# First mixer of a two-layer trunk: the convolution's input in PSUM, one of its blocks in the first pass, fourteen taps on ScalarE

## The chip, the core and the metric

One NeuronCore of a Trainium2 chip. The metric is the device time of one execution in microseconds (us). Five engines run side by side, each through its own instructions in order: TensorE (PE, matmuls), VectorE (DVE), ScalarE (ACT), GpSimd (POOL) and SyncE (SP), whose queue issues the DMA loads. SBUF holds operands; PSUM holds what TensorE writes, in eight banks of 128 partitions by 512 floats.

## The reference, cut to what matters

Two layers over 256 tokens of width 2048. Each layer: a modulation vector, a mixer, an output projection, a feed-forward network. The change lies in the mixer of layer 0:

```python
def even_mixer(h, ...):
    z = h @ w_in
    a, q, kc, vc, ks, vs, kw, vw, gl = split_cols(z, EVEN_SPLITS)
    y_a = conformer_conv(a, conv_w, conv_b, conv_ln_g, conv_ln_b)
    y_b = nsa_attention(q, kc, vc, ks, vs, kw, vw, gl, cos, sin, positions, ...)
    return jnp.concatenate([y_a, y_b], axis=-1) @ w_out

def conformer_conv(a, w_dw, b_dw, ln_g, ln_b):
    a1, a2 = jnp.split(a, 2, axis=-1)
    y = causal_dwconv(a1 * jax.nn.sigmoid(a2), w_dw, b_dw)     # 31 taps, one filter per channel
    return jax.nn.silu(layer_norm(y, ln_g, ln_b))
```

The attention has 8 query heads of 128 in 2 groups; queries and keys are normalised (a root per head and token), scaled and rotated (rope). `mod = silu(c) @ ada_w + ada_b` gives the modulation.

## The kernel before

**Tiles.** The contraction over 2048 runs as 16 tiles of 128 (`kt`). Weights come through three SBUF buffers named `raw`, in the order in which `W.want` listed them; `W.take` hands out the next and loads ahead. In the first mixer all products are fp32; such a product shows as two records in the trace.

**The first pass** (the loop over `kt` at the end of the setup) makes, for each `kt`, the compressed keys' input (`oc`, 2 products of 256 columns), the keys (`ok`) and the first four query heads for both key groups (`oq`), 6 products of 512 columns. Two rows of the modulation matrix (`ada`, 1 MB each) are loaded and reduced on VectorE beside each `kt`.

**After it**, in program order: four *fills*, two products `ev_v` (values and gate logits), two `ev_c` (the compressed values' input), a compression network `hidden(0)`, two fills, `hidden(1)`, and then attention with nine more fills and one spare take. A fill is one 256-column projection over all 16 `kt`, half of a convolution block; a *pair* of fills is a block of 128 channels, of which there are 8. The first fill of a pair goes through `tanh` on ScalarE into `sg`; with the second, `taps` writes the gated block `xp = (sg + 1) * o`, padded by 30 columns.

**The convolution.** Block `c` has 31 taps, in jobs of four VectorE taps (`PER`). ScalarE multiplies `TAPS_ACT` of the 31 shifted views by their weights into `pr`, GpSimd adds these into `yp`; VectorE accumulates the others into `y` and `ye`. `xp` lies in SBUF, in two buffers. Every `take` runs `hook` (the next step of attention or of the heads) and `tick`, which emits jobs and modulation rows by the rates `CONV_*` and `ADA_*`. The position of each in the engines' streams is thus set when the program is built, and each engine goes through its stream in order.

**The heads.** `squares(i)` sums the squares of the keys (i = 0) and of the two halves of the first four heads' banks on ScalarE, `roots` takes the 24 roots at once on VectorE, `scaled(i)` multiplies, `roped(i)` rotates (two of four steps on GpSimd, `rope`'s `rest` on VectorE), `turned_in(i)` transposes on TensorE (L613) into `KT` and `qT`, from within `ev_v`.

**Attention**, for head `hd`: scores (L1142, L1145), their maxima on VectorE (`weights`, L1157 to L1165), exponentials on ScalarE, the factors of the sums (L1179 to L1182), transposes (L1194), copies to SBUF (`pT` L1198 on VectorE, L1199 and L1200 on ScalarE), the product with the values (L1205, L1209). Three heads are under way at a time, each step a hook, and half a fill lies between the steps.

**The end of the mixer** (`out_first`): projection with the weights `out`, first over the attention's half of the mix; meanwhile the convolution's last blocks are finished, `centre` and `layer_stats` (L986, L987) and `layer_scale` (L408, L409) give its layer norm, and then the convolution's half follows. The modulation rows go through two buffers `ada`: the load of row n waits in SP's queue until VectorE has reduced row n - 2, and the weight loads behind it wait with it.

Of the kernel before, what the change touches and what calls it, by code (L numbers as in the profile page):

```python
# [16 lines left out]
P = 128  # L17
# [29 lines left out]
TAPS_ACT = 10  # L47
TAPS_LAST = 9
# [6 lines left out]
LO_A = 0.25  # L55
ADA_A = 0.25
CONV_A = 0
CONV_1 = 0.7
CONV_2 = 2.0
CONV_3 = 1.2  # L60
# [8 lines left out]
ADA_T = 0.4  # L69
LO_F = 0.25  # L70
ADA_1 = 0.5
ADA_2 = 0.5
ADA_3 = 0.6
# [6 lines left out]
ADA_OUT = 0.45  # L80
# [72 lines left out]
def trunk(ctx, tc, a, out):  # L153
# [9 lines left out]
    psum = ctx.enter_context(tc.tile_pool(name="psum", bufs=8, space=bass.MemoryType.PSUM))  # L163

    def bank():
        return psum.tile([P, 512], F32, tag="bank", name="bank")

# [39 lines left out]
    for kt in range(KD):  # L207
        W.want(a["ev_1"][kt], 1, 1792, cuts=(768, 1024), split=False)
# [9 lines left out]
    want_pairs(0, 2)  # L218
    for c in range(2):
        W.want(a["ev_v"][c], KD, 268, split=False)  # L220
    for g in range(2):
        W.want(a["ev_c"][g], KD, P, split=False)
    want_hidden(0)
    want_pairs(2, 3)
    want_hidden(1)
    want_pairs(3, 8)
# [506 lines left out]
    V.memset(onesm, 1.0)  # L733
    make_identity(nc, ident)
# [38 lines left out]
    oc = [bank()[:, :T] for _ in range(2)]  # L773
    ok = [bank() for _ in range(NT)]
    oq = [[bank() for _ in range(NT)] for _ in range(2)]
    for kt in range(KD):
        x = h(kt)
        if kt > 1:
            next(table, None)
        first, stop = kt == 0, kt == KD - 1  # L780
        w, _ = take()
        for g in range(2):
# [14 lines left out]
    with tc.tile_pool(name="l0", bufs=2) as lp:  # L797
# [84 lines left out]
        xps = [lp.tile([P, 30 + T], F32, name=f"xp{u}", bufs=1) for u in range(2)]  # L882
        for xp in xps:
            G.memset(xp[:, :30], 0.0)
# [3 lines left out]
        def fill():  # L888

            o = proj_t(h)  # L890
# [130 lines left out]
        def roots():  # L1021
            flat = s24.rearrange("p a b -> p (a b)")
            V.tensor_scalar(flat, flat, 1.0 / P, EPS, op0=ALU.mult, op1=ALU.add)
            r = rsqrt(flat, 24)
            V.tensor_scalar(r[:, 8:], r[:, 8:], SCALE, None, op0=ALU.mult)
            root.append(r)

        def scaled(i):
# [3 lines left out]
            for t in range(NT):  # L1032
                u = 2 * i + t
                head_scale(zs[u], 4, root[0][:, 4 * u:4 * u + 4], gain, n[:, t])
# [21 lines left out]
        hooks.append(lambda: (squares(0), adds[0]()))  # L1056
        hooks.append(lambda: (squares(1), adds[1]()))
        hooks.append(lambda: (squares(2), masks()))
        hooks.append(roots)
        hooks.append(lambda: scaled(0))  # L1060
        hooks.append(lambda: (scaled(1), roped(0)))
        hooks.append(lambda: (scaled(2), roped_rest()))
        hooks.append(lambda: roped(1))
        hooks.append(lambda: (turned_in(0), roped_rest()))
        hooks.append(lambda: roped(2))
        hooks.append(lambda: (turned_in(1), roped_rest()))
        hooks.append(None)
        hooks.append(lambda: turned_in(2))
        rate.update(ada=ADA_A, jobs=CONV_A)
        W.share = LO_A  # L1070
        for _ in range(4):
            fill()
# [14 lines left out]


# [5 lines left out]
        for g in range(2):  # L1094
            o = proj_t(h)
            defer(lambda g=g, o=o: hooks.append(windows(1, g, o)))
# [142 lines left out]
        for _ in range(9):  # L1239
# [10 lines left out]
        def ready(c):  # L1250
# [3 lines left out]
            if c < 7:  # L1254
# [4 lines left out]
                                      lambda: (normed(1), activated(0))], ready, ADA_OUT)  # L1259

# [233 lines left out]
def layout(inputs):  # L1494
# [51 lines left out]
    a["ev_1"] = np.concatenate([s["kc"], s["ks"], s["kw"], s["q"]], axis=1).reshape(KD, P, 1792)  # L1546
# [45 lines left out]
```

## Time and profile before

| what | us |
|---|---|
| median of 3 runs | 2399.79 (2398.73 to 2402.48) |
| the profiled execution, and its span | 2407.39, 2405.7 |
| TensorE busy in the span | 2305.6 (96%) |
| first pass on TensorE | 31.62 to 140.96 |
| from there to the first scores | 140.96 to 286.15 |
| attention, to the first product of `out` | 286.15 to 386.49 |
| end of the mixer, to the feed-forward network | 386.49 to 516.53 |

TensorE is busy nearly all of the span, so the places of interest are those where it waits, and the stretches after such waits in which its matmuls take longer. In a list of the instructions in order of time, the value in brackets at a row's end is how long the engine stood idle just before it, and behind the arrow who ended that; merged rows give a count (x), and the duration covers all of them.

### The profile page before, as it was taken

Reading aid. Unit: us, or ns where it says so; the run is one execution under the profiler, and the core shown is the slowest. Engines: PE = TensorE matmul, PEld = TensorE weight load, DVE = VectorE, ACT = ScalarE, POOL = GpSimd, SP = SyncE. Lnnn points to the kernel's source line nnn. Section 1 sums busy time; section 2 is a strip of 40 time slices with the busy share of each in tenths; the row PEclk is TensorE's granted clock in tenths of the full one; section 3 lists DMA queues with packets and bytes.
Section 4 is the critical chain, followed back from the end, with each engine's and each line's share of the span. In section 5 each row is a group of like instructions: output and inputs, shape, how many; then the busy total and the mean of one; then the engine's idle time right before and its main releaser. Section 6 shows DMA issues by size and latency. Waiting matters only on the chain. (4 is left out here: it accounts for less than half of the span.)

```text
span 2405.7 us, 39971 instructions
## 1 busy us (share of the span) xinstructions
PE 2305.6 (96%) x16056; PEld 2133.9 (89%) x16056; DVE 1669.6 (69%) x2611; ACT 1028.5 (43%) x1803; POOL 527.5 (22%) x309
## 2 busy tenths in 40 slices
PE   6898999998999999999999999999999999999999
PEld 3476777888999999999999877999999999999999
DVE  7758689738968877877888467665686554554554
ACT  2021254125434544544544555446534444444443
POOL 4233534001312222222222010000222212222221
PEclk9999999999999999999999999999999999999999
DMA  9968754866878888878887543444577545545545
GB/s 381 427 223 340 291 192 175 294 237 258 322 282 330 331 298 333 328 289 312 333 316 269 199 175 123 153 175 167 217 276 266 187 157 203 184 159 205 181 166 168
DMA packets 96381, 596.62 MB, mean 248 GB/s; under 512 B 11457, under 2 KB 14145, under 8 KB 44097
## 3 DMA queue, kind: packets, MB, share of 16 engines
q1 hardware_dynamic: 96194, 594.06, 66.6%
q8 instruction: 126, 2.06, 0.3%
q14 instruction: 61, 0.50, 0.1%
HBM read 591.92 MB, written 2.10 MB: 247 GB/s over the span
## 5 line engine op out<-in xcount | busy, mean ns | idle before, releaser
L133 ACT ACTIVATE whi<-raw 128x1024 fp32r<-128x1024 f32 (+2 forms) x659 | 626.1, 951 | 856.1 <-PE bank L347 716.2
L139 DVE TENSOR_TENSOR wlo<-raw,whi 128x1024 fp32r<-128x1024 f32 (+1 forms) x515 | 585.4, 1138 | 410.2 <-ACT whi L133 409.8
L348 PE MATMUL bank<-h,wlo 128*128 128x256 f32 x2624 | 745.0, 284 | 12.3 <-DVE wlo L139 11.4
L346 PE MATMUL bank<-h,whi 128*128 128x256 f32 x2624 | 744.8, 284 | 0.2 <-ACT whi L133 0.2
L347 PE MATMUL bank<-h,whi 128*128 128x256 f32 x2624 | 743.8, 283 | 0.0
L139 POOL TENSOR_TENSOR wlo<-raw,whi 128x1024 fp32r<-128x1024 f32 (+2 forms) x144 | 339.9, 2360 | 1484.0 <-ACT whi L133 1439.5
L348 PEld LDWEIGHTS bank<-h,wlo 128*128 128x128 f32 x2624 | 505.0, 192 | 14.0 <-DVE wlo L139 12.6
L346 PEld LDWEIGHTS bank<-h,whi 128*128 128x128 f32 x2624 | 505.2, 193 | 0.5 <-ACT whi L133 0.5
L347 PEld LDWEIGHTS bank<-h,whi 128*128 128x128 f32 x2624 | 505.2, 193 | 0.1
L269 DVE CUSTOM_DVE_ANT_0 ada<-ada,cB,adab 128x2048 f32<-128x2048 f32 x192 | 464.9, 2425 | 29.6 <-DMA ada<-adaw 28.9
L347 PE MATMUL bank<-g,whi 128*128 128x256 f32 x1408 | 403.7, 287 | 9.7 <-DVE g L662 9.6
L346 PE MATMUL bank<-g,whi 128*128 128x256 f32 x1408 | 403.4, 287 | 7.6 <-ACT g L661 7.2
L348 PE MATMUL bank<-g,wlo 128*128 128x256 f32 x1408 | 404.1, 287 | 5.5 <-DVE wlo L139 4.1
L347 PEld LDWEIGHTS bank<-g,whi 128*128 128x128 f32 x1408 | 274.6, 195 | 11.3 <-DVE g L662 11.3
L346 PEld LDWEIGHTS bank<-g,whi 128*128 128x128 f32 x1408 | 274.7, 195 | 8.6 <-ACT g L661 7.8
L348 PEld LDWEIGHTS bank<-g,wlo 128*128 128x128 f32 x1408 | 274.7, 195 | 8.1 <-DVE wlo L139 5.4
L350 PE MATMUL bank<-hw,raw 128*128 128x256 f32 x640 | 150.6, 389 | 13.1 <-DMA raw<-ev 7.5
L350 PEld LDWEIGHTS bank<-hw,raw 128*128 128x128 f32 x640 | 121.9, 194 | 42.3 <-issue 18.6
L650 DVE SCALAR_TENSOR_TENSOR y<-bank,fcw,y 128x255 f32<-128x255 f32 x162 | 77.4, 478 | 96.8 <-ACT y L649 96.8
L350 PE MATMUL bank<-hr,raw 128*128 128x257 f32 x640 | 140.4, 380 | 0.0
L350 PEld LDWEIGHTS bank<-hr,raw 128*128 128x128 f32 x640 | 121.0, 190 | 16.6
L350 PE MATMUL bank<-mixw,raw 128*128 128x256 f32 x512 | 119.0, 396 | 5.5 <-DMA raw<-out 5.5
(263 smaller groups left out, 2469.9 us busy)
## 6 DMA issues: line engine op xcount, KB each, us to landing
ada<-adaw SPq DMA_DIRECT2D x192, 1024.0 KB, 5.7
raw<-wup SPq DMA_DIRECT2D x162, 1024.0 KB, 6.3
raw<-wdn SPq DMA_DIRECT2D x128, 704.0 KB, 4.3
raw<-out SPq DMA_DIRECT2D x44, 512.0 KB, 3.6
raw<-ev_a SPq DMA_DIRECT2D x16, 1024.0 KB, 5.4
raw<-ev SPq DMA_DIRECT2D x16, 896.0 KB, 14.7
raw<-wup SPq DMA_DIRECT2D x16, 896.0 KB, 4.6
raw<-cmp_w SPq DMA_DIRECT2D x8, 1024.0 KB, 9.2
```

The lines of the kernel that those rows point to most:

```text
L133: nc.scalar.activation(hi[:, :n], raw, AF.Copy)
L139: eng.tensor_sub(lo[:, :n], raw, hi[:, :n].bitcast(F32))
L269: V.tensor_tensor_reduce(w, w, cB, 1.0, adab[:, i * 96 + j:i * 96 + j + 1], ALU.mult, ALU.add, m)
L346: PE.matmul(o, hi[:, s_], x[:, 0], start=start, stop=False)
L347: PE.matmul(o, hi[:, s_], x[:, 1], start=False, stop=False)
L348: PE.matmul(o, lo[:, s_], x[:, 0], start=False, stop=stop)
L350: PE.matmul(o, w[:, s_], x, start=start, stop=stop)
L650: V.scalar_tensor_tensor(y[:, 1:], o[:, :T - 1], w[:, 1:2], y[:, 1:], op0=ALU.mult, op1=ALU.add)
```

## The change

- The first pass makes one convolution block too: its weights (`ev_1`) are 2048 columns wide, not 1792, and `oc` has four parts, two of the compressed keys and two of a pair of fills. These lie two to a bank, so a bank is first set by a product of zeros. The first of the two banks comes from a new pool `xq` of one bank; the other seven are `psum0`.
- `xp` is one buffer in the bank of `xq`, no longer two in SBUF: `taps` of block c waits until the jobs of block c - 1 are all emitted, and both VectorE and ScalarE read the taps from PSUM.
- 14 taps of each block go to ScalarE and GpSimd (12 for the last), where it was 10 (9); VectorE has 17 (19) instead of 21 (22).
- The roots are taken by parts (`roots(0)`, `roots(1)`, `roots(2)`), the keys' at once after the first pass.
- After the first pass come `ev_c`, `ev_v` with the transposes, `hidden(0)`, one pair, `hidden(1)`, and twelve fills around and beside attention. `W.load_to(kt + 2)` puts the load of a pass's weights ahead of that iteration's modulation rows in SP's queue.
- Rates of jobs and modulation rows are other numbers. After the mixer `all_banks` gives the feed-forward network eight banks again.

```diff
-TAPS_ACT = 10
-TAPS_LAST = 9
+TAPS_ACT = 14
+TAPS_LAST = 12
...
-CONV_1 = 0.7
-CONV_2 = 2.0
-CONV_3 = 1.2
+CONV_1 = 0.6
+CONV_2 = 1.0
+CONV_3 = 2.0
...
-    psum = ctx.enter_context(tc.tile_pool(name="psum", bufs=8, space=bass.MemoryType.PSUM))
+    banks = [tc.tile_pool(name="xq", bufs=1, space=bass.MemoryType.PSUM),
+             tc.tile_pool(name="psum0", bufs=7, space=bass.MemoryType.PSUM)]
+    xq, psum = [p.__enter__() for p in banks]
...
-        W.want(a["ev_1"][kt], 1, 1792, cuts=(768, 1024), split=False)
+        W.want(a["ev_1"][kt], 1, 2048, cuts=(1024, 1024), split=False)
...
-    oc = [bank()[:, :T] for _ in range(2)]
+    oc = [xq.tile([P, 512], F32, tag="xp", name="oc"), bank()]
+    for o in oc:
+        PE.matmul(o, zero[:, :P], zero, start=True, stop=False)
+    oc = [o[:, u * T:(u + 1) * T] for o in oc for u in range(2)]
...
     for kt in range(KD):
+        W.load_to(kt + 2)
         x = h(kt)
...
-        for g in range(2):
-            mm_t(oc[g], w, slice(g * P, (g + 1) * P), x, first, stop)
-        mm_n(ok, w, slice(256, 768), x, first, stop)
+        for g in range(4):
+            mm_t(oc[g], w, slice(g * P, (g + 1) * P), x, False, stop and g % 2 == 1)
+        mm_n(ok, w, slice(512, 1024), x, first, stop)
...
-            while c > 1 and c - 2 not in tapped:
+            while c and c - 1 not in tapped:
                 jobs.pop(0)()
-            xp = xps[c % 2]
+            if not xps:
+                xps.append(xq.tile([P, 512], F32, tag="xp", name="xp")[:, :30 + T])
+                V.memset(xps[0][:, :30], 0.0)
+            xp = xps[0]
...
+        fill(oc[2])
+        fill(oc[3])
+        advance()
+        squares(0)
+        advance()
+        roots(0)
+        scaled(0)
+        hooks.append(lambda: squares(1))
+        hooks.append(lambda: (roots(1), scaled(1)))
+        hooks.append(lambda: (squares(2), adds[0]()))
+        hooks.append(lambda: (roots(2), scaled(2)))
...
-        for _ in range(9):
+        for _ in range(11):
             fill()
...
+    drain()
+    all_banks()
```

Three places in the engines' streams. In the rows `hw` is the layer's input, `raw` a weight buffer, `n` the scaled keys or heads.

TensorE, from the end of the first pass to the first compression network, before:

```order
L361 MATMUL bank<-raw,hw 128x512 x6
L350 MATMUL bank<-hw,raw 128x256 x64
L613 MATMUL bank<-ident,n 128x128 x8
L361 MATMUL bank<-raw,hw 128x268 x8
L613 MATMUL bank<-ident,n 128x128 x8
L361 MATMUL bank<-raw,hw 128x268 x10
L613 MATMUL bank<-ident,n 128x128 x8
L361 MATMUL bank<-raw,hw 128x268 x46
L350 MATMUL bank<-hw,raw 128x256 x32
```

The same stretch after:

```order
L366 MATMUL bank<-raw,hw 128x512 x6
L355 MATMUL bank<-hw,raw 128x256 x32
L366 MATMUL bank<-raw,hw 128x268 x22
L618 MATMUL bank<-ident,n 128x128 x8
L366 MATMUL bank<-raw,hw 128x268 x6
L618 MATMUL bank<-ident,n 128x128 x8
L366 MATMUL bank<-raw,hw 128x268 x4
L618 MATMUL bank<-ident,n 128x128 x8
L366 MATMUL bank<-raw,hw 128x268 x32
```

The 64 products of four fills are gone from here and 32 of `ev_c` stand in their place; behind them 22 products of `ev_v` come ahead of the first transposes, where there were none.

VectorE, the first taps beside attention, with the engines that each instruction waits for, before:

```order
L904 SCALAR_TENSOR_TENSOR xp_581<-sg,bank 128x256 [waits PE_49]
L926 TENSOR_SCALAR cy<-xp_581,cvw 128x256 [waits DVE_49]
L928 TENSOR_SCALAR ye<-xp_581,cvw 128x256
L930 SCALAR_TENSOR_TENSOR cy<-xp_581,cvw,cy 128x256 [waits DVE_49]
L930 SCALAR_TENSOR_TENSOR ye<-xp_581,cvw,ye 128x256 [waits DVE_49]
L930 SCALAR_TENSOR_TENSOR cy<-xp_581,cvw,cy 128x256 [waits DVE_49]
```

The same place after, on VectorE and then on ScalarE:

```order
L918 SCALAR_TENSOR_TENSOR xp<-sg,bank 128x256 [waits PE_49]
L940 TENSOR_SCALAR cy<-xp,cvw 128x256 [waits DVE_49,Activation_49]
L942 TENSOR_SCALAR ye<-xp,cvw 128x256
L944 SCALAR_TENSOR_TENSOR cy<-xp,cvw,cy 128x256 [waits DVE_49]
L944 SCALAR_TENSOR_TENSOR ye<-xp,cvw,ye 128x256 [waits DVE_49]
L944 SCALAR_TENSOR_TENSOR cy<-xp,cvw,cy 128x256 [waits DVE_49,Activation_49]
```

```order
L933 ACTIVATE yp<-xp,cvw 128x256 [waits DVE_49]
L933 ACTIVATE pr<-xp,cvw 128x256 [waits Pool_49] x2
L933 ACTIVATE pr<-xp,cvw 128x256 [waits DVE_49,Pool_49]
L933 ACTIVATE pr<-xp,cvw 128x256
L933 ACTIVATE pr<-xp,cvw 128x256 [waits Pool_49]
```

The first tap of every four on VectorE now waits for ScalarE, and the first of every three on ScalarE for VectorE, where only the writing of `xp` was waited for.

VectorE, the end of the layer norm in `out_first` (`layer_stats`, then `layer_scale`), before:

```order
L402 SCALAR_TENSOR_TENSOR rsy<-rst,rsy 128x2
L994 TENSOR_TENSOR mz<-mz,rsy 128x2
L408 TENSOR_SCALAR diag<-ident,rsy 128x128 x2
L408 TENSOR_SCALAR diag<-ident,mz 128x128 x2
L1005 TENSOR_TENSOR cy<-cy,bank 128x256
```

After:

```order
L407 SCALAR_TENSOR_TENSOR rsy<-rst,rsy 128x2
L1008 TENSOR_TENSOR mz<-mz,rsy 128x2
L274 ISA ada,mod<-ada,cB,adab 128x2048
L274 ISA mod 128x1
L413 TENSOR_SCALAR diag<-ident,rsy 128x128 x2
L413 TENSOR_SCALAR diag<-ident,mz 128x128 x2
```

A modulation row moved in between the roots and the diagonals that TensorE takes.

## Rows read from the trace of the kernel before

**Rows 1.** Waits of TensorE, 20 to 520 us: total, times, longest

```profile
PE bank L350 <- DMA raw<-ev: 7.5, 9, 1.2
PE bank L866 <- DVE hs L861: 3.0, 1, 3.0
PE bank L613 <- DVE n L606: 2.6, 2, 2.2
PE bank L849 <- DMA raw<-cmp_w: 2.2, 2, 1.5
PE bank L361 <- DMA raw<-ev_v: 1.6, 1, 1.6
PE bank L350 <- DMA raw<-ev_c: 1.5, 1, 1.5
```

**Rows 2.** TensorE in order of time, first pass: start, duration, engine, instruction, [idle before]

```profile
31.62 2.07 PE L350 MATMUL bank<-hw,raw 128*128 128x256 f32 x4 [3.54 <-ACT hw L511]
...
40.79 1.03 PE L350 MATMUL bank<-hw,raw 128*128 128x256 f32 x4
...
134.94 1.03 PE L350 MATMUL bank<-hw,raw 128*128 128x256 f32 x4
...
140.96 27.79 PE L350 MATMUL bank<-hw,raw 128*128 128x256 f32 x128
```

**Rows 3.** First pass, busy us by engine; last three columns: clock, DMA share, GB/s

```profile
40.00:125.00 85.00, 77.42 (x202) 37.30 (x201) 69.43 (x82) 8.91 (x16) 35.47 (x21) 1.00 1.01 426
```

**Rows 4.** TensorE in order of time, behind the last of the heads' transposes

```profile
182.99 19.92 PE L361 MATMUL bank<-raw,hw 128*128 128x268 f32 x84
```

**Rows 5.** VectorE in order of time: root step, modulation row, scalings, rope step

```profile
151.75 0.18 DVE L397 TENSOR_SCALAR rsi<-s 128x24 int32<-128x24 int32 x1
...
154.21 2.34 DVE L269 CUSTOM_DVE_ANT_0 ada<-ada,cB,adab 128x2048 f32<-128x2048 f32 x1
...
156.82 6.29 DVE L596 SCALAR_TENSOR_TENSOR n<-bank,rsy,gains 128x128 f32<-128x128 f32 x24
163.02 0.68 DVE L605 TENSOR_TENSOR n<-n,cc 128x512 f32<-128x512 f32 x1
```

**Rows 6.** ScalarE in order of time, ahead of the second compression network's turn

```profile
270.86 0.51 ACT L919 ACTIVATE pr<-xp,cvw 128x256 f32<-128x256 f32 x1 [2.22 <-POOL yp L921]
```

**Rows 7.** VectorE in order of time, taps and one head's step beside attention

```profile
293.52 0.94 DVE L930 SCALAR_TENSOR_TENSOR cy<-xp,cvw,cy 128x256 f32<-128x256 f32 x1
...
303.50 0.48 DVE L930 SCALAR_TENSOR_TENSOR cy<-xp,cvw,cy 128x256 f32<-128x256 f32 x1
303.89 0.48 DVE L930 SCALAR_TENSOR_TENSOR ye<-xp,cvw,ye 128x256 f32<-128x256 f32 x1
...
312.61 0.68 DVE L1198 COPY pT<-bank 128x512 f32<-128x512 f32 x1
...
316.71 0.48 DVE L930 SCALAR_TENSOR_TENSOR cy<-xp,cvw,cy 128x256 f32<-128x256 f32 x1
```

**Rows 8.** ScalarE in order of time, two copies out of PSUM

```profile
305.64 0.36 ACT L1199 ACTIVATE pT<-bank 128x256 f32<-128x256 f32 x1
305.90 0.36 ACT L1200 ACTIVATE pC<-bank 15x256 f32<-15x256 f32 x1
```

**Rows 9.** TensorE in order of time, attention

```profile
313.34 1.25 PE L1209 MATMUL bank<-pT,vn 128*128 128x128 f32 x8 [2.98 <-DVE pT L1198]
314.38 5.26 PE L350 MATMUL bank<-hw,raw 128*128 128x256 f32 x16
...
342.06 1.08 PE L1142 MATMUL bank<-KT,qT 128*128 128x271 f32 x4
...
365.08 1.08 PE L1142 MATMUL bank<-KT,qT 128*128 128x271 f32 x4
```

**Rows 10.** TensorE in order of time, end of the mixer

```profile
414.19 13.51 PE L350 MATMUL bank<-mixw,raw 128*128 128x256 f32 x48 [3.36 <-DMA raw<-out]
430.61 0.56 PE L986 MATMUL bank<-onesm,cs 128*128 128x1 f32 x2 [2.91 <-DVE cs L979]
```

More of the change, by code (lines that the diff above doesn't have):

```diff
@@ L68 @@
 LO_T = 0.25
-ADA_T = 0.4
+ADA_T = 0.6
 LO_F = 0.25
-ADA_1 = 0.5
-ADA_2 = 0.5
-ADA_3 = 0.6
+ADA_1 = 0.45
+ADA_2 = 0.45
+ADA_3 = 0.55
 ADA_F0S = 0.45
@@ L79 @@
 CONV = 1.6
-ADA_OUT = 0.45
+ADA_OUT = 0.55
 LO_L1 = 0.0
@@ L216, in want_hidden @@
             W.want_raw(a["cmp_w1"][kv, :, u * 2048:(u + 1) * 2048], 2048)
-    want_pairs(0, 2)
+    for g in range(2):
+        W.want(a["ev_c"][g], KD, P, split=False)
     for c in range(2):
         W.want(a["ev_v"][c], KD, 268, split=False)
-    for g in range(2):
-        W.want(a["ev_c"][g], KD, P, split=False)
     want_hidden(0)
-    want_pairs(2, 3)
+    want_pairs(1, 2)
     want_hidden(1)
-    want_pairs(3, 8)
+    want_pairs(2, 8)
     want_out(0)
@@ L733, in trunk @@
     V.memset(onesm, 1.0)
+    zero = hm.tile([P, 512], F32, tag="hm", name="zero")
+    V.memset(zero, 0.0)
     make_identity(nc, ident)
@@ L881, in trunk, with fill @@
         glu = []
-        xps = [lp.tile([P, 30 + T], F32, name=f"xp{u}", bufs=1) for u in range(2)]
-        for xp in xps:
-            G.memset(xp[:, :30], 0.0)
+        xps = []
         norm = {}
         count, totals, tapped = [0], [], set()
-        def fill():
-            o = proj_t(h)
+        def fill(o=None):
+            if o is None:
+                o = proj_t(h)
             if count[0] % 2 == 0:
@@ L1033, in scaled @@
                 u = 2 * i + t
-                head_scale(zs[u], 4, root[0][:, 4 * u:4 * u + 4], gain, n[:, t])
+                head_scale(zs[u], 4, root[i][:, 4 * t:4 * t + 4], gain, n[:, t])
         later = []
@@ L1054, in turned_in @@
                     S.activation(qT[i - 1][:, :, t * P:(t + 1) * P], p, AF.Copy)
[L1056 to L1072, printed above, removed]
         rate.update(ada=ADA_1, jobs=CONV_1)
         W.share = LO_1
+        fill(oc[2])
[9 more added lines that the diff above has]
+        hooks.append(lambda: (roots(2), scaled(2)))
+        hooks.append(lambda: (roped(0), adds[1]()))
+        hooks.append(lambda: (roped_rest(), roped(1)))
+        hooks.append(lambda: (roped_rest(), roped(2)))
+        hooks.append(lambda: (roped_rest(), masks()))
+        beside.extend([None] * 9)
+        for i in range(3):
+            beside.append(lambda i=i: turned_in(i))
         vn = lp.tile([P, NT, 536], F32, name="vn", bufs=1)
@@ L1086, in gates @@
             V.tensor_scalar(g_, g_, 1.0, None, op0=ALU.add)
+        for g in range(2):
+            o = proj_t(h)
+            defer(lambda g=g, o=o: hooks.append(windows(1, g, o)))
         for c in range(2):
```

23 lines of the change are left out of this document (11 added, 12 removed).

## Prediction

> **What bounds the kernel now.** I read the list of TensorE's waits first, then the instructions of each engine in order of time around each wait. TensorE does the same work before and after, but for two products of zeros: each convolution block still costs two fills, wherever they stand. So the change is worth only what it does to TensorE's idle time and to the slower matmuls that follow it, nearly all of it in the first mixer, up to 516 us. The waits of that part [rows 1] fall into four kinds: weights of the first pass (7.5 us in 9 waits), weights of the products behind it (2.2 + 1.6 + 1.5), VectorE's rotated keys and heads (2.6), and VectorE's or ScalarE's lateness around the convolution (3.0 in rows 1, 2.98 in rows 9, 2.91 in rows 10, with 3.36 for the weights `out`).
>
> What a wait costs beyond itself is read from what follows it. The 128 records from 140.96 take 27.79 us [rows 2], so 16 take 3.5 and 48 take 10.4. Behind the wait of 2.98, 16 took 5.26 [rows 9], 1.8 more; behind the wait of 3.36, 48 took 13.51 [rows 10], 3.1 more. I take 2 us for each wait of about 3.
>
> **First pass.** One 256-column product is 27.79 / 64 = 0.43 us, so a pair of fills is 32 x 0.43 = 13.9 us, and that much leaves the stretch behind the pass. It comes back as two products in each of 16 steps. A step without a wait takes 140.96 - 134.94 = 6.02 us [rows 2]; now 6.9. From 31.62 a pass that never waits would end at 31.62 + 16 x 6.9 + 3.1 = 145.1, where 3.1 is what the first step lost (40.79 - 31.62 = 9.17 against 6.02). The products of zeros stand in the 3.54 idle ahead of it and may save that: 142.0. The DMAs are full in this stretch, 426 GB/s at a share of 1.01 [rows 3], and 2.1 MB more to bring take 4.9 us: 145.9 if they set the end. But loading ahead of the modulation rows gives each step's weights a whole step more. I take 143.9, so 2.9 later with 13.9 less behind: **-11**. Ends: -13 (142.0) and -7 (nothing gained by the new order, every product behind the DMAs).
>
> **Keys and heads.** After the pass TensorE has 13.9 us of `ev_c` and 22 products of 268 columns (0.45 each by width) until it wants the keys, 23.8 us after the pass. It was 27.6 us of fills before the first transposes. VectorE now passes, counted from the end of the pass: three root chains of 12, 13 and 13 steps at 0.2 (7.6), 24 scalings at 0.262 (6.3), eight taps (3.2), two additions for the compression (about 1 each), two modulation rows (4.7), the keys' rope (4 x 0.65 = 2.6) [rows 5, 7]. That is 26.4, so keys 2.6 late; GpSimd beside it can make that 4, if it slows a rope step as it slows taps [rows 7]. The first heads need 4 taps and a rope more and come as they are wanted; the second need another 4 taps, a modulation row and a rope (6.5) while TensorE has about 3.7 us of work: 2.5 late. With slower matmuls behind two waits that is 8 to 9, against 2.6 and about 1 (84 records of 268 columns took 19.92 [rows 4], 19.1 by width) before: **+4.5**, ends +2 and +8.
>
> **Weights behind the pass.** `ev_c` is now partly loaded before the pass ends, and less TensorE work stands behind it per byte. The 5.3 us of rows 1 may vanish or stay: **-3**, ends -5.3 and 0.
>
> **The second network's turn** (L866, 3.0 late). VectorE waits for ScalarE's `hs`, which stands behind ScalarE's taps, and those wait for GpSimd (2.22 [rows 6]): GpSimd's additions and VectorE's taps from SBUF slow each other (a tap takes 0.94 beside them, 0.48 alone [rows 7]). With `xp` in PSUM a tap has one SBUF input left. I take the short price throughout, and the 17.7 us that TensorE has between the pair and the turn then hold all jobs: **-4** of 3.0 + 1.8, ends -4.8 and 0. [...] No run so far shows a tap from PSUM.
>
> **Attention.** A pair of heads is 23.0 us on TensorE (342.06 to 365.08 [rows 9]). VectorE has in it two heads' steps of 4.1 (312.61 to 316.71 [rows 7]), 17 taps at 0.40, `xp` and the last addition (0.8), and two modulation rows (4.7): 20.5. With 21 taps, most at 0.9, it was over 23, and late by 2.98 in the first pair. But the order shows a new wait: each four taps of VectorE wait for three of ScalarE, and these for the four before. Three out of PSUM take 0.26 + 0.26 + 0.36 = 0.9 [rows 8]; so VectorE stands still about 1.0 in three jobs that come in a row, 0.8 in the last, and up to 2 more where ScalarE is at exponentials: 24.3 to 26.3 for a pair, 28 where a third row falls in. What queues behind the waiting taps is the copy `pT`, for which TensorE waits. Four pairs overrun by 5 to 6 us in all, with less lost behind them than behind one long wait, against 2.98 + 1.8: **+1**, ends -4.8 and +9.
>
> By the Trainium skill (PSUM — Partial Sum Buffer, PSUM bank collisions raise a hardware error) two engines may not touch one bank and quadrant at once, two reads included, and dependencies keep them apart: these are the waits in the order. Were reads free to overlap, this term would be -4.8.
>
> **End of the mixer.** Before: 3.36 + 3.1 and 2.91 + 2. A last fill now follows attention; counted from its end, TensorE has ten steps of 3.5 until `layer_stats` at 34.7. VectorE writes the last `xp` about 4 us after, goes through five jobs with turns and one row (13.5), and with sums and four rows (9.4 to 11) has the last `cs` at 30 to 32. So 2.91 goes. The ninth load of `out` waits for the second of those four rows, at about 23.5, and is wanted at 27.5; its load and the rows' before it take 4 to 5: about 1 late. New is the row between roots and diagonals: roots 2.7 and row 2.34 against one step of 3.5, a wait of 1.5 to 2 and what follows it. Sum 5 where it was 11.4: **-6.5**, ends -11 and 0. A drain at the change of pools adds **+0.7**, one eviction's length, ends 0 and 1.
>
> Rows of the modulation shift by a take in the feed-forward network, where VectorE is also short: 0, ends -3 and +3.
>
> **Sum.** -11 + 4.5 - 3 - 4 + 1 - 6.5 + 0.7 = -18.3. The profiled execution's 2407.4 would be 2389; it lies 7.6 above the median, so I set the sum against the median 2399.8: **2382**.
>
> **Rivals.**
> 1. *The turns at the bank make VectorE the bound of attention* (slower). If ScalarE's taps stand behind a head's exponentials and scalings (3.8 us) in two more jobs of each pair, three pairs pay 7.6 more each and lose 2 behind it: +29, so 2411. For it: ScalarE's taps and the heads' steps share one queue, and one `xp` lets no block run ahead. Against it: most jobs stand next to each other in both streams. It decides once scores of heads two apart come over 25 us apart where rows 9 show 23.0. Chance 0.13.
> 2. *The gains behind the pass don't come*: weights, turn and end of the mixer cost as before, because the same modulation rows hold SP's queue and `cs`: 2382 + 3 + 4 + 6.5 = 2395.5, about level. For it: four rows stand together ahead of the last `cs`. Chance 0.17.
> 3. *The pass pays for its pair*: loads stay behind and 4 us more are lost there: 2386. Chance 0.17.
> 4. *VectorE has the room that the taps free* and no wait is left in attention or at the heads: -5.8 and -3 more, 2373. Chance 0.10.
>
> My forecast has 0.43. About 0.2% (4.8 us) is what a measurement here can tell from no change. Faster than 2395: forecast, rivals 3 and 4 and nearly half of rival 2, 0.74. Within 2395 to 2404.6: the rest of rival 2 and the edge of others, 0.13. Slower: 0.13, rival 1. The range: from 2368, a little beyond rival 4, to 2403, past rival 2; rival 1 is left out with most of its chance, and some below.
>
> **What would show it.** The first pass ends at 142 to 146 and its waits for `ev` are under 3 us. Behind it the transposes wait twice, 2 to 4 us each, for VectorE's `n`. Taps from PSUM take 0.48 beside GpSimd's additions; if 0.94, attention and the end fall with them. The wait before L878 is gone. Each first of four taps stands still about 1 us for ScalarE's `pr`; scores two heads apart come 23 to 25 us apart. `layer_stats` waits for nothing, the diagonals behind it 1.5 to 2. I am wrong most simply if those turns cost over 2 us each.

## The result, and the profile after

The changed kernel takes 2419.5 us (median, 2411.5 to 2430.8) where the kernel before, run beside it, takes 2400.4 (2398.2 to 2403.3): a ratio of 1.0087, 95% interval 1.0071 to 1.0103. It is 19 us slower by the medians, 17 to 25 by the interval; 2382 was predicted. Its profiled execution took 2418.8, its span is 2417.1.

The kernel before was also profiled a second time, among the experiments (e5): 2393.9, span 2392.1. The profile on which the prediction stood (2407.4) was thus a long execution of it, and the table sets the change against both. In both columns the pair of fills that moves (13.9 us of records) is counted where it now stands, so that the rows show time and not work: 13.9 less is allowed for in the pass, 13.9 more in attention, and between them 27.8 of fills are gone.

| stretch | after, us | against the first profile | against the second | forecast |
|---|---|---|---|---|
| first pass, to its end | ends 144.46 | -10.4 | -9.2 | -11 |
| from there to the first scores | 128.43 | +11.0 | +10.3 | -2.5 (4.5 - 3 - 4) |
| attention | 134.86 | +20.6 | +22.3 | +1 |
| end of the mixer | 123.54 | -6.5 | -1.7 | -6.5 |
| all behind it | 1885.8 | -3.4 | +3.3 | +0.7 |
| sum | | +11.3 | +25.0 | -18.3 |

(The first row: 144.46 - 140.96 - 13.9; the third: 134.86 - 100.34 - 13.9.) The two stretches in the middle carry the loss. TensorE's waits of the kernel after, the same list as [rows 1], those that are new or have changed most:

```profile
PE bank L618 <- DVE n L611: 13.7, 6, 6.1
...
PE bank L1210 <- ACT sc L1203: 10.4, 2, 8.1
PE bank L1210 <- ACT mixw L1227: 7.5, 4, 3.6
...
PE bank L355 <- DMA raw<-out: 4.2, 3, 1.6
PE bank L861 <- DMA raw<-cmp_w: 3.7, 1, 3.7
```

What [rows 1] held is mostly gone: no wait for `ev` in the pass (7.5 before), none for `ev_v` and `ev_c`, and for `hs` ahead of L878 0.4 instead of 3.0. In their place TensorE waits 13.7 us for VectorE's rotated keys and heads (2.6 before), and 17.9 for ScalarE in attention, where such waits were of 0.5 before.

The first pass went as forecast. TensorE in order of time there, and the window that answers to [rows 3], columns as there:

```profile
32.34 2.08 PE L355 MATMUL oc<-hw,raw 128*128 128x256 f32 x4 [0.86 <-ACT hw L516]
...
41.31 1.03 PE L355 MATMUL oc<-hw,raw 128*128 128x256 f32 x4
...
144.46 13.98 PE L355 MATMUL bank<-hw,raw 128*128 128x256 f32 x64
```

```profile
40.00:125.00 85.00, 85.00 (x250) 47.22 (x249) 64.90 (x76) 7.81 (x13) 34.31 (x19) 1.00 1.00 417
```

TensorE is busy in all 85.00 us, where it stood still in 7.6 of them before. In the nine kernels below that have this pass it ended earlier still, at 141.7 to 142.9: their first step took 6.98 to 7.71 us, where it took 8.97 (41.31 - 32.34) in this profile.

**Attention.** ScalarE of the kernel after, one block's taps (`pr`, L933) in order of time, with the exponentials and scalings of a head (L1189, L1203) behind them:

```profile
281.40 1.20 ACT L933 ACTIVATE pr<-xp,cvw 128x256 f32<-128x256 f32 x3 [1.85 <-DVE ye L944]
284.39 1.20 ACT L933 ACTIVATE pr<-xp,cvw 128x256 f32<-128x256 f32 x3 [1.78 <-POOL yp L935]
...
287.38 1.20 ACT L933 ACTIVATE pr<-xp,cvw 128x256 f32<-128x256 f32 x3 [1.51 <-POOL yp L935]
295.24 0.84 ACT L933 ACTIVATE pr<-xp,cvw 128x256 f32<-128x256 f32 x2 [6.66 <-DVE ye L944]
...
296.23 0.41 ACT L1189 ACTIVATE sc<-sc,nm 128x128 f32<-128x128 f32 x1
...
298.56 1.49 ACT L1203 ACTIVATE sc<-sc,su 128x128 f32<-128x128 f32 x4
```

VectorE of the same stretch, in order of time:

```profile
282.64 0.48 DVE L944 SCALAR_TENSOR_TENSOR cy<-xp,cvw,cy 128x256 f32<-128x256 f32 x1 [1.33 <-ACT pr L933]
...
285.62 0.48 DVE L944 SCALAR_TENSOR_TENSOR cy<-xp,cvw,cy 128x256 f32<-128x256 f32 x1 [1.33 <-ACT pr L933]
...
287.20 2.34 DVE L274 CUSTOM_DVE_ANT_0 ada<-ada,cB,adab 128x2048 f32<-128x2048 f32 x1
...
289.47 0.43 DVE L1173 TENSOR_TENSOR sc<-bank,cm 128x271 f32<-128x271 f32 x1
...
293.49 0.48 DVE L944 SCALAR_TENSOR_TENSOR cy<-xp,cvw,cy 128x256 f32<-128x256 f32 x1
...
296.11 0.48 DVE L944 SCALAR_TENSOR_TENSOR cy<-xp,cvw,cy 128x256 f32<-128x256 f32 x1 [0.97 <-ACT pr L933]
```

And TensorE:

```profile
289.39 1.08 PE L1158 MATMUL bank<-KT,qT 128*128 128x271 f32 x4
...
299.01 0.77 PE L1210 MATMUL bank<-ident,sc 128*128 128x128 f32 x2 [8.11 <-ACT sc L1203]
...
301.01 4.42 PE L355 MATMUL bank<-hw,raw 128*128 128x256 f32 x16
...
310.89 1.08 PE L1158 MATMUL bank<-KT,qT 128*128 128x271 f32 x4
```

Read the three together. At 288.6 ScalarE has done twelve of its 14 taps, and the last two come next. They read the bank that VectorE's fourth job reads, and stand behind that job; VectorE comes to it at 293.49, after a modulation row and a head's maxima and factors. So ScalarE stands still for 6.66 us with that head's exponentials behind it in its queue, and TensorE, which wants the scaled scores behind these, for 8.11. Not all of it is the turn's: the head's maxima were ready at 291.5, and the exponentials began at 296.23, 4.7 later. It happens again at 323.79 (7.08). VectorE's own stops, 1.33 each, look small beside it; e11 below tests whether they are.

**Keys and heads.** VectorE, behind the first pass, in order of time:

```profile
160.31 0.65 DVE L405 TENSOR_TENSOR rst<-rsy 128x8 f32<-128x8 f32 x1
...
163.43 0.17 DVE L405 TENSOR_TENSOR rst<-rsy 128x8 f32<-128x8 f32 x1
...
177.47 0.48 DVE L944 SCALAR_TENSOR_TENSOR cy<-xp,cvw,cy 128x256 f32<-128x256 f32 x1 [3.17 <-ACT pr L933]
...
185.36 0.48 DVE L944 SCALAR_TENSOR_TENSOR cy<-xp,cvw,cy 128x256 f32<-128x256 f32 x1 [3.17 <-ACT pr L933]
```

Both stops of 3.17 stand ahead of the heads' rope. They come from a ring, three engines that wait for each other: VectorE's tap waits for ScalarE's `pr`, that waits for GpSimd to add the one before (7.48 and 4.78 us of standing still on ScalarE there), and GpSimd's additions stand behind its four rope steps of the part before, 172.72 to 176.22 and 180.54 to 184.13. TensorE, in order of time:

```profile
172.72 0.90 PE L618 MATMUL bank<-ident,n 128*128 128x128 f32 x4 [4.35 <-DVE n L611]
...
190.84 1.09 PE L618 MATMUL bank<-ident,n 128*128 128x128 f32 x4 [6.07 <-DVE n L611]
```

It waits 4.35 for the keys, ahead of both stops, and 6.07 for the second heads, behind them. From the end of the pass up to the keys' rope VectorE does not stand still at all; but seven small steps of the roots (148.42 to 163.00) take 0.58 to 0.68 us, each beside an instruction of GpSimd, where others take 0.17.

### The profile page after: what moved, and what is told of

Read it like the earlier page. It is cut to its first block, busy times and chain, and to the rows that moved or that the text cites. A ratio compares the mean times of both kernels' runs of the same rounds, so it can differ in the third digit from the quotient of the medians.

```text
span 2417.1 us, 40125 instructions
## 1 busy us (share of the span) xinstructions
PE 2307.0 (95%) x16060; PEld 2133.7 (88%) x16060; DVE 1649.2 (68%) x2607; ACT 1037.3 (43%) x1834; POOL 532.0 (22%) x338
## 5 line engine op out<-in xcount | busy, mean ns | idle before, releaser
L136 DVE TENSOR_TENSOR wlo<-raw,whi 128x1024 fp32r<-128x1024 f32 (+1 forms) x515 | 592.5, 1152 | 411.0 <-ACT whi L130 410.9
L353 PE MATMUL bank<-h,wlo 128*128 128x256 f32 x2624 | 746.1, 284 | 13.3 <-DVE wlo L136 9.9
L136 POOL TENSOR_TENSOR wlo<-raw,whi 128x1024 fp32r<-128x1024 f32 (+2 forms) x144 | 350.6, 2435 | 1483.3 <-ACT whi L130 1445.5
L274 DVE CUSTOM_DVE_ANT_0 ada<-ada,cB,adab 128x2048 f32<-128x2048 f32 x192 | 471.7, 2459 | 41.0 <-DMA ada<-adaw 40.2
L352 PE MATMUL bank<-g,whi 128*128 128x256 f32 x1408 | 401.8, 285 | 11.4 <-DVE g L667 11.2
L355 PE MATMUL bank<-hw,raw 128*128 128x256 f32 x576 | 137.4, 392 | 0.6 <-DMA raw<-ev_a 0.6
L355 PEld LDWEIGHTS bank<-hw,raw 128*128 128x128 f32 x576 | 112.0, 198 | 18.2 <-issue 1.4
L355 PE MATMUL bank<-mixw,raw 128*128 128x256 f32 x512 | 113.1, 382 | 6.1 <-DMA raw<-out 4.2
```

What stands on the lines that cost most here:

```text
L136: eng.tensor_sub(lo[:, :n], raw, hi[:, :n].bitcast(F32))
L274: V.tensor_tensor_reduce(w, w, cB, 1.0, adab[:, i * 96 + j:i * 96 + j + 1], ALU.mult, ALU.add, m)
L352: PE.matmul(o, hi[:, s_], x[:, 1], start=False, stop=False)
L353: PE.matmul(o, lo[:, s_], x[:, 0], start=False, stop=stop)
L355: PE.matmul(o, w[:, s_], x, start=start, stop=stop)
```

## The experiments

The theories at the start: **the turns** (two engines that may only read `xp` one after the other hold each other's queues up) and **the contention** (the taps, where they read SBUF, run against GpSimd). A third is that the loss lies in one block's `xp` no longer running ahead (**the single buffer**, rival B in what was expected). The median of the kernel before lay between 2396 and 2401 in all comparisons.

| run | us | ratio to before, 95% interval |
|---|---|---|
| e1 ScalarE's own copy in SBUF | 2395.4 | 0.9973 to 1.0001 |
| e2 one `xp` in SBUF for both | 2421.5 | 1.0063 to 1.0142 |
| e3 after, 10 and 9 taps | 2406.9 | 1.0026 to 1.0056 |
| e4 before, `xp` in a bank | 2414.5 | 1.0048 to 1.0104 |
| e5 before, profile again | 2393.9 | one execution |
| e6 before, 14 and 12 taps | 2402.6 | 1.0009 to 1.0039 |
| e7 after, two `xp` in SBUF | 2420.0 | 1.0075 to 1.0115 |
| e8 e1 and no early jobs | 2379.8 | 0.9907 to 0.9954 |
| e9 after, no early jobs | 2406.2 | 1.0005 to 1.0052 |
| e10 e8 with 10 and 9 taps | 2379.3 | 0.9880 to 0.9926 |
| e11 after, taps in four jobs | 2414.1 | 1.0045 to 1.0095 |
| e12 e9, taps in four jobs | 2402.8 | 0.9997 to 1.0032 |

**e1: the turns taken away.** VectorE writes the gated block twice, `xp` into the bank for itself and `xa` into SBUF for ScalarE.

```diff
+                xps.append(lp.tile([P, 30 + T], F32, name="xa", bufs=1))
...
+            V.scalar_tensor_tensor(xa[:, 30:], sg, 1.0, o, op0=ALU.add, op1=ALU.mult)
+            V.scalar_tensor_tensor(xp[:, 30:], sg, 1.0, o, op0=ALU.add, op1=ALU.mult)
...
-                    S.activation(pr, xp[:, j:j + T], AF.Copy, scale=cvw[:, c, j:j + 1])
+                    S.activation(pr, xa[:, j:j + T], AF.Copy, scale=cvw[:, c, j:j + 1])
```

> The changed kernel, but ScalarE reads its taps from a copy of xp in SBUF that VectorE writes too (one instruction of 0.43 us more per block); VectorE still reads the bank. No turns are left. Theory T (the two engines' turns at the bank, and the heads' exponentials queued on ScalarE behind a tap that waits for VectorE, cost the time): VectorE's waits for pr in attention fall from about 1.3 us in three jobs a block to under 0.3, the waits of TensorE for ScalarE's sc and mixw (17.9 us) to under 5, attention from 134.9 to 115 to 119 us, total 2393 to 2403. Rival G (14 taps are too many for ScalarE and GpSimd, wherever xp lies): attention stays over 130 us, total 2412 to 2425. Rival B (one xp buffer lets no block run ahead): the same as G.

24 us less than after. Attention is 115.25 (134.86 after; before's 100.34 and the pair make 114.2). TensorE's waits for ScalarE there are 1.9 (at the place where it was 8.11) and 2.1:

```profile
PE bank L618 <- DVE n L611: 9.8, 4, 4.5
...
PE bank L618 <- ACT KT L1071: 2.1, 1, 2.1
PE bank L1214 <- ACT mixw L1231: 2.1, 2, 1.0
PE bank L1214 <- ACT sc L1207: 1.9, 1, 1.9
```

The groups of taps on VectorE and ScalarE, 260 to 420 us (shapes, count, busy us, mean ns, and after the bar the idle time before them and what ended it), of after and then of e1:

```profile
L944 DVE SCALAR_TENSOR_TENSOR cy<-xp,cvw,cy 128x256 f32<-128x256 f32 x46 | 22.0, 478 | 20.7 <-ACT pr L933 20.7
...
L940 DVE TENSOR_SCALAR cy<-xp,cvw 128x256 f32<-128x256 f32 x6 | 3.3, 544 | 8.6 <-ACT pr L933 8.6
...
L933 ACT ACTIVATE pr<-xp,cvw 128x256 f32<-128x256 f32 x74 | 30.0, 469 | 47.7 <-DVE ye L944 32.1 <-POOL yp L935 15.6
```

```profile
L948 DVE SCALAR_TENSOR_TENSOR cy<-xp,cvw,cy 128x256 f32<-128x256 f32 x49 | 23.2, 473 | 0.0
...
L937 ACT ACTIVATE pr<-xa,cvw 128x256 f32<-128x256 f32 x76 | 36.2, 502 | 23.1 <-POOL yp L939 22.6 <-POOL cs L992 0.2
```

With the copy VectorE's 20.7 and 8.6 us of standing still are gone, and ScalarE's 32.1 for VectorE's `ye`. So nearly the whole loss in attention is the turns: of its 19.6 us TensorE's waits make 14.3 (18.5 against 4.2), and the slower matmuls behind them the rest (busy for 116.3 us against 111.1). e1 still has one `xp` for each reader and seven banks for the rest, so the single buffer and the lost bank are not the cause.

At the heads the copy brings little. VectorE's two stops of 3.17 are gone, but TensorE still waits 9.8 us for `n` and 2.1 for ScalarE's copy of the keys (`KT`), which stands behind ScalarE's taps; from the pass to the first scores it takes 124.8 instead of 128.4.

**e2: no turns, but `xp` in SBUF.** One buffer, read by both engines.

```diff
-                xps.append(xq.tile([P, 512], F32, tag="xp", name="xp")[:, :30 + T])
+                xps.append(lp.tile([P, 30 + T], F32, name="xps", bufs=1))
```

> The changed kernel with xp, still one buffer, in SBUF for both engines. Theory T: no turns, but VectorE's taps and GpSimd's additions meet again (taps of 0.94 where GpSimd adds), so less is won than with the copy: attention 118 to 128 us, total 2400 to 2412. Rival G: total 2412 to 2430. Rival B: as the changed kernel, within 5 us, since one buffer is left.

A miss: without turns it is as slow as after. In attention it took 124.9, as expected; against e1 it loses 9.7 there, 7.2 between the pass and the first scores, and 9.2 at the end of the mixer. VectorE's taps, 260 to 420 us (minimum, median, maximum in ns):

```profile
L944 DVE SCALAR_TENSOR_TENSOR ye<-xps,cvw,ye x43: 472/943/1006, 280.1 to 419.8; 128x256 f32<-128x256 f32 x43
```

In after the same line shows 472, 474 and 477. From SBUF most taps take twice as long. Of 87 taps that stand singly between 262 and 418 us all 56 of over 0.7 us lie beside an instruction of GpSimd, and the 27 beside none take at most 0.52; in after 65 of 85 lie beside one, and none is slowed. The contention costs here in all what the turns cost, at other places: the change traded one for the other, and e1 has neither at its taps. That agrees with the Trainium skill (SBUF — State Buffer, Who interferes with whom): outside its two-port modes (which copies, casts and tensor-scalar steps can enter) a VectorE instruction with at most one input in SBUF does not contend with GpSimd, and one with two contends with a GpSimd instruction that reads SBUF.

**e3: the changed kernel with 10 and 9 taps on ScalarE.**

```diff
-TAPS_ACT = 14
-TAPS_LAST = 12
+TAPS_ACT = 10
+TAPS_LAST = 9
```

> The changed kernel with 10 taps of a block (9 of the last) on ScalarE, as before the change; xp stays in PSUM. Theory T: the turns stay (six jobs instead of five, two ScalarE taps each), VectorE has four taps more: waits of TensorE for ScalarE's sc and mixw stay over 12 us, total 2412 to 2430. Rival G: those waits fall under 5, total 2398 to 2408. Rival B: within 5 us of the changed kernel.

The waits for ScalarE stay, 9.2 and 8.1 us, as the turns demand; the total is 5 lower than expected. That came at the heads: the waits for `n` are 8.1 instead of 13.7, from the pass to the first scores it takes 121.9 instead of 128.4, and VectorE has none of the stops of 3.17 there. Attention takes 132.8.

**e4: the kernel before with `xp` in a bank**, and seven banks for the rest. Nothing else of the change is in it but what this needs: the two pools, and `drain` and `all_banks` behind the mixer.

```diff
-            while c > 1 and c - 2 not in tapped:
+            while c and c - 1 not in tapped:
...
-            xp = xps[c % 2]
+            if not xps:
+                xps.append(xq.tile([P, 512], F32, tag="xp", name="xp")[:, :30 + T])
+                V.memset(xps[0][:, :30], 0.0)
+            xp = xps[0]
```

> The kernel before with nothing changed but xp: one buffer in a bank of its own, seven banks for the rest. Theory T: turns come into a stream that is otherwise that of before, six jobs a block: VectorE idle about 1 us in each for ScalarE's pr, TensorE waits for ScalarE's sc or mixw over 8 us, total 2410 to 2430. Rival G: 2396 to 2404, no more than before. Rival B: 2405 to 2415 with no waits of VectorE for pr.

16 us slower than before, as expected. The new waits are the same kind as in after: `mixw` 9.7 (once), `sc` 8.8, `n` 10.4. The bank, with one buffer and seven banks for the rest, brings a loss of this size without any other part of the change; that neither the one buffer nor the seven banks are the cause is shown by e1, which keeps both.

**e5: the kernel before once more**, for the spread of its profile; no edit.

> The kernel before, a second profiled execution: the first one took 2407.4 us, above all timed runs of it (2392 to 2406). If its excess lies in the first mixer, the stretch up to 516.5 us is 4 to 8 us shorter here and the sum was made against a slow first pass; if it lies behind, that stretch ends at 515 to 518 again and the rest, 1889 us, is shorter. Either way 2394 to 2403.

Used in the table above. The end of the mixer took 125.24, not 130.04: the wait for `cs` was there (4.1), but a wait for `out` of 2.09 was not, and the records behind the waits were quicker.

**e6: the kernel before with 14 and 12 taps on ScalarE.** `xp` stays in SBUF.

```diff
-TAPS_ACT = 10
-TAPS_LAST = 9
+TAPS_ACT = 14
+TAPS_LAST = 12
```

> The kernel before with 14 taps of a block on ScalarE and GpSimd (12 of the last) and nothing else. Four VectorE taps fewer a block and four additions of GpSimd more, all from SBUF. Theory C (GpSimd's additions and VectorE's taps hold each other up when both read SBUF): what VectorE saves in number it loses as more of its taps take 0.94 instead of 0.48: 2396 to 2412. If taps only count by number, VectorE has 1.6 to 3.8 us less a block and the waits of 2.98 and 2.91 vanish: 2386 to 2394.

Not faster, though VectorE has 31 taps fewer: from 286 to 420 us a tap now takes 0.77 on average where it took 0.66 (55.9 us for 73 taps, 61.1 for 92). Of the 12.6 us of 19 taps, 7.4 come back through the contention, and attention takes 100.2 (100.3 and 98.7 before). The waits for `out` grow to 10.5.

**e7: after, `xp` in SBUF, two buffers.**

```diff
-            while c and c - 1 not in tapped:
+            while c > 1 and c - 2 not in tapped:
...
-                xps.append(xq.tile([P, 512], F32, tag="xp", name="xp")[:, :30 + T])
...
+                xps.append(lp.tile([P, 30 + T], F32, name=f"xps{c}", bufs=1))
...
+            xp = xps[c % 2]
```

> The changed kernel with xp in SBUF in two buffers, as before the change: tells what the one buffer costs in the run with xp in SBUF (2421.5). Theory C: it is the contention of taps and additions, the second buffer brings under 6 us, 2414 to 2424. Rival B (one buffer holds the blocks up): 2396 to 2410.

Within 1.5 us of e2: the second buffer is worth nothing here either, and the single buffer, which e1 had spoken against, falls as a theory. e6 has the same taps in SBUF in the order of before and is 17 us faster. The early jobs (13 to 16 us, e8 and e9) may be most of that; no run has late jobs with `xp` in SBUF.

**e8 and e9: no jobs of the convolution ahead of the heads.** The rate of jobs is 0 until the second product `ev_v` has been emitted, behind all of the heads' transposes; e8 is e1 with it, e9 the changed kernel with it.

```diff
-        rate.update(ada=ADA_1, jobs=CONV_1)
+        rate.update(ada=ADA_1, jobs=0.0)
...
         for c in range(2):
             o = proj_n(268, h)
             defer(lambda o=o, c=c: values(o, c))
+            rate.update(jobs=c * CONV_1)
```

> The run with ScalarE's copy of xp, with the first block's taps kept out of the way of the heads: no jobs before the second product of values. VectorE then has eight taps less ahead of the rotated keys and heads, and GpSimd no additions ahead of their rope steps. TensorE's waits there, 9.8 + 2.1 us, fall to 3 to 7; total 3 to 8 us under the run with the copy (2387 to 2393 on its chip), faster than both kernels. If the waits stay over 9, the taps were not what delayed the heads.

> The changed kernel, xp in the bank for both engines, with no jobs before the second product of values. Apart from the turns in attention, which stay, this takes away the first block's taps that stood between the heads' steps: TensorE's waits at the heads' transposes (13.7 us) fall to 3 to 6, as in the run with copy and late jobs (3.6); attention keeps its 17 to 18 us of waits for ScalarE. Total 8 to 15 us under the changed kernel: 2404 to 2412, still slower than before. If turns in attention were not a cost of their own, it would come out near 2385.

e8 is 16 us below e1, more than expected, and 0.7% below the kernel before. e9 lies in its range, and its waits at the heads' transposes fall to 4.7, those for ScalarE in attention stay at 18.3. Together the four kernels are a square:

| | jobs early | jobs late | difference |
|---|---|---|---|
| turns at the bank | after 2419.5 | e9 2406.2 | -13.3 |
| copy in SBUF | e1 2395.4 | e8 2379.8 | -15.6 |
| difference | -24.1 | -26.4 | |

The four were not timed side by side; by their ratios to the kernel before, taken beside each, the differences are -14 both times for the jobs, -24 and -23.5 for the turns. Both costs are there, each by itself, and mostly in their own stretches. From the pass to the first scores after takes 128.43 and e1 124.77, e9 115.87 and e8 113.37: the early jobs cost 11 to 13 us there, the turns 3 to 4. Attention takes 134.86 and 134.62 with turns, 115.25 and 115.24 without. In e8 the waits at the heads are small; the list of its TensorE waits:

```profile
PE bank L355 <- DMA raw<-out: 4.4, 2, 3.6
PE bank L618 <- DVE n L611: 3.6, 3, 2.6
PE bank L861 <- DMA raw<-cmp_w: 3.4, 1, 3.4
```

**e10: e8 with 10 and 9 taps.** The edit is e3's.

> The run with copy and late jobs, with 10 taps of a block on ScalarE and GpSimd (9 of the last), as before the change. If 14 taps are worth something once turns and contention are gone, VectorE is the short engine again in attention and at the end of the mixer: 1.6 us a block, 5 to 12 us slower, 2385 to 2392. If VectorE has room enough, within 4 us of 2380.

2379.3 beside 2379.8: with neither turns nor contention VectorE's taps cost 0.47 each, it has the room for them, and the 14 taps bring nothing that can be measured.

**e11 and e12: ScalarE's taps in the first four jobs of a block**, on after and on e9, so that nothing of ScalarE's stands behind VectorE's fourth job (the 6.66 us above).

```diff
-                a0, a1 = (-(-len(acts) * u // njobs) for u in (n, n + 1))
+                a0, a1 = (-(-len(acts) * min(u, njobs - 1) // (njobs - 1)) for u in (n, n + 1))
```

> The changed kernel, with ScalarE's taps in the first four of a block's five jobs (4, 3, 4, 3 instead of 3, 3, 3, 3, 2; the last block the like): the turns at the bank stay, but ScalarE has nothing left in a block's last job, so it no longer waits for VectorE's fourth job. In the changed kernel that wait was 6.66 and 7.08 us in the two places looked at, with a head's exponentials behind it, and TensorE then stood 8.11 us for ScalarE. If the price of the turns is paid in ScalarE's queue, TensorE's waits for ScalarE between the scores and the transposes (10.4 + 7.5 us) fall to 4 to 11 and the time to 2403 to 2413. If it is VectorE's own stops at the bank (20.7 us in 17 stops in attention) that make it, the waits move by under 3 and the time stays within 5 of 2419.5.

> The same edit on the kernel of e9 (2406.2: turns kept, no tap job ahead of the second product ev_v). If ScalarE's queue is the place, attention gets shorter by 7 to 14 and the time is 2392 to 2401; if VectorE's stops are, 2402 to 2410. The kernel without turns (e8) was 2379.8, so whatever remains above it is what the turns cost at other places.

The explanation by the last group alone falls: e12 lies in the range that was expected if VectorE's stops are the place, and e11 half a us outside it; e11's waits for ScalarE fall by 2.0, where 7 to 14 would go if ScalarE's queue were the place. ScalarE's stops of over 4 us are gone, and all its standing still before taps in attention falls from 47.7 us to 23.8, which is e1's 23.1. Yet the time falls by only 5 and 3, the intervals overlapping, and attention by 1.7 (133.18) and 0.6 (134.01). TensorE's waits in e11:

```profile
PE bank L1210 <- ACT mixw L1227: 12.3, 3, 4.3
...
PE bank L1210 <- ACT sc L1203: 3.5, 1, 3.5
```

The wait for the scaled scores falls from 10.4 to 3.5, and the one for `mixw` rises from 7.5 to 12.3. ScalarE and then TensorE of e11, in order of time:

```profile
335.26 1.20 ACT L933 ACTIVATE pr<-xp,cvw 128x256 f32<-128x256 f32 x3 [1.85 <-DVE ye L944]
338.25 1.57 ACT L933 ACTIVATE pr<-xp,cvw 128x256 f32<-128x256 f32 x4 [1.79 <-POOL yp L935]
339.69 0.40 ACT L1227 ACTIVATE mixw<-bank 128x256 f32<-128x256 f32 x1
```

```profile
340.14 1.11 PE L1210 MATMUL bank<-ident,sc 128*128 128x128 f32 x4 [4.33 <-ACT mixw L1227]
```

The block's taps, with 1.85 of waiting for VectorE's `ye` and 1.79 for GpSimd's `yp`, hold ScalarE from 331.85 to 339.7, and now it is the copy of a head's output (`mixw`) that stands behind them, whose bank TensorE wants. The groups of e11, as those of after and e1 above:

```profile
L944 DVE SCALAR_TENSOR_TENSOR cy<-xp,cvw,cy 128x256 f32<-128x256 f32 x48 | 22.9, 477 | 18.0 <-ACT pr L933 18.0
...
L940 DVE TENSOR_SCALAR cy<-xp,cvw 128x256 f32<-128x256 f32 x6 | 3.3, 544 | 10.7 <-ACT pr L933 10.7
...
L933 ACT ACTIVATE pr<-xp,cvw 128x256 f32<-128x256 f32 x76 | 30.1, 469 | 23.8 <-DVE ye L944 12.5 <-POOL yp L935 11.3
```

VectorE's stops for `pr` are what did not change, with the first tap of each block (L940, L944): 29.3 us in after (20.7 + 8.6), 28.7 in e11 (18.0 + 10.7), 0.2 in e1. So the loss went with the turns as a whole, not with the place of one of them. How much of the 24 us is paid in VectorE's queue and how much in ScalarE's stays open: the two go through a block in step, and no run has the stops on one engine only.

## Why the prediction was wrong

**First pass: right.** -10.4 and -9.2 against -11; it ended at 144.46 for 143.9. The full DMAs (rival 3) did not hold it up: TensorE never waited for `ev`, though there was more to load. What the products of zeros may save, they mostly did, though not in this profile: the first step, 6.88 without a loss, took 8.97 here and 6.98 to 7.71 in the nine other kernels with this pass, whose ends (141.7 to 142.9) lie at the 142.0 that I had as the best case.

**Weights and the second network's turn: right in the main.** The waits for `ev_v` and `ev_c` and the one ahead of L878 went; the one for `cmp_w` grew from 2.2 to 3.7, and 0.6 for `ev_a` is new. As waits that is -1.0 (3.1 gone, 2.1 added) and -2.6, where -3 and -4 stood with what follows them.

**Keys and heads: the term that was mis-sized, 4.5 for some 15.** The 26.4 us of VectorE's work up to the keys took 29.8 (144.46 to 174.30), without a stop: the seven slowed steps make 3.3 of the difference. So TensorE waited 5.2 for the keys, where 2.6 to 4 was forecast, 1.3 for the first heads, where nothing was, and 7.3 for the second, where 2.5 was. Behind the keys stand VectorE's two stops of 3.17 for ScalarE's taps, which stand behind GpSimd's additions, which stand behind GpSimd's rope; I had weighed the turns in attention alone. But these are the smaller part: e1 has no such stops and is only 3.7 us shorter there. The larger part is that the first block's jobs are there at all, on three engines. Without them (e9) the stretch is 12.6 us shorter, and against the first profile of before, with the fills allowed for, it comes to -1.5, near the -2.5 of the forecast. Which engine's share of these jobs costs how much no run separates.

**Attention: the step that failed, +1 for +21.** What I expected of a tap was right: 0.474 from PSUM beside GpSimd. VectorE's stops were right in sum: 1.33 and 0.97 where 1.0 and 0.8 stood (ScalarE's three taps took 1.20 out of PSUM, not 0.9), and 8.6 in all at the blocks' first taps, which I had left out; that is 29.3 us for six blocks, 4.9 each, where I had 3.8 to 5.8. The step that failed is what I did with them: I added them to VectorE's work, compared that with TensorE's 23.0 us for a pair of heads, and named the copy `pT` as all that stands behind a stop. A turn has two ends. ScalarE waits too, at times for all that VectorE has between two jobs (6.66), and behind ScalarE stand a head's exponentials, its scalings and the copy of its output. TensorE waits for these (17.9 us), and VectorE then waits for TensorE's transposes (4.8 us ahead of `pT`). In such a ring the sums of the single engines do not give the time: VectorE was busy for 100.5 of the 134.9 us in which I feared that it would be full. e1 shows the size of it, 19.6 us of attention; how it divides between the two queues stays open (e11).

The Trainium skill (PSUM — Partial Sum Buffer, PSUM bank collisions raise a hardware error) says that dependencies keep two engines' reads of a bank apart, and the trace agrees: VectorE stood 29.3 us for `pr` and ScalarE 32.1 for `ye`. What that costs was mine to price.

Rival 1 is the nearest to what came, with another mechanism: it had ScalarE's taps behind a head's exponentials and VectorE as the bound, where the exponentials stood behind the taps and VectorE was idle for a quarter of the stretch. Its sign showed: the last three scores of heads two apart, 22.6 to 23.0 us apart before, come 26.2 to 30.4 apart in after (the two ahead of them were over 25 before, too, and are no sign). Its chance of 0.13 was too low for a wait that I had read in the order but in no trace. My own sign of being wrong, turns of over 2 us each, looked at VectorE alone: none of its stops in attention is longer than 1.81, but five of ScalarE's for VectorE are over 3.

**End of the mixer: the number met against the first profile by luck.** TensorE in order of time, after, and then the one wait of before that [rows 10] leave out:

```profile
437.05 3.69 PE L355 MATMUL bank<-mixw,raw 128*128 128x256 f32 x16 [1.51 <-DMA raw<-out]
442.33 3.69 PE L355 MATMUL bank<-mixw,raw 128*128 128x256 f32 x16 [1.59 <-DMA raw<-out]
...
452.38 2.06 PE L414 MATMUL bank<-diag,onesm 128*128 128x128 f32 x8 [2.01 <-DVE diag L413]
...
478.03 14.08 PE L355 MATMUL bank<-mixw,raw 128*128 128x256 f32 x64 [1.91 <-DVE xT L543]
493.20 38.25 PE L355 MATMUL bank<-mixw,raw 128*128 128x256 f32 x176 [1.09 <-DMA raw<-out]
```

```profile
487.14 29.55 PE L350 MATMUL bank<-mixw,raw 128*128 128x256 f32 x128 [2.09 <-DMA raw<-out]
```

`layer_stats` waits for nothing, and the diagonals behind it 2.01, as forecast. But the loads of `out` wait 1.51 and 1.59 where about 1 was forecast, and 1.91 for `xT` and 1.09 for `out` were not in the sum at all. At the rate of [rows 2] the stretch's 512 records take 111.2 us, and the layer norm's own products some 3. What is left is lost: 16 us in the first profile of before, 11 in the second, 9.5 in after, where I had 11.4 before and 5 after. So the term after was too small by half, and the -6.5 came out only because the first profile had lost more than I counted. Subtracting the 7.6 from the sum corrects its base, not this term.

**The price behind a wait**, 2 us for each of about 3, came from one execution. In the second profile 16 records behind the same wait of 2.98 took 3.62 us, no more than without a wait, and behind one of 3.09 they took 6.49.

**The sum.** From the pass to the first scores the forecast was 13 too low, in attention 20 to 21, at the end of the mixer 0 to 5, in the pass 1 to 2, and the rest, by the two profiles, is 4 shorter to 3 longer. That turns the forecast's -18 into +11 by the one profile and +25 by the other; the medians are 19 apart.

## What to carry to other kernels

When two engines must take turns at a buffer, price both queues: for each engine what it waits for at each turn, and what stands behind the waiting instruction there. A wait is as long as what the *other* engine has in its queue before its turn ends, not as long as the turn itself. A buffer moved to where a contention ends may need a second copy for the other reader: here one more write of 0.42 us for each block was worth 24 us. And where a change moves jobs to the front of a program, price what they put into each engine's queue ahead of the work that TensorE wants next: here the first block's jobs ahead of the heads cost 13 to 16 us.

## What the runs showed that was not expected

- VectorE's taps with one input in PSUM were never slowed beside GpSimd (472 to 485 ns over 86 of them); with both in SBUF the median was 943. The contention also reaches small instructions: 128x8 root steps took 0.58 to 0.68 instead of 0.17 us, among them tensor-scalar steps with one tensor input in SBUF (0.68 at 148.42). No run shows in which mode these ran.
- The contention of 14 taps on ScalarE and GpSimd (e2) and the turns at the bank (after) cost the same within 2 us, though at different places, so the trade looked like no effect until both were taken away.
- Two profiled executions of the kernel before, 13.6 us apart in their spans, differ by 4.8 us in the end of the mixer: the wait for `cs` is longer in the shorter one (4.1 for 2.9), but it lacks one wait for `out` (2.09), and its records are quicker (48 in 12.28 us for 13.51).
